# A four-layer network on one core: the first projection gets its own code, and table work on GpSimd is queued later

## The chip, the core and the metric

The kernel runs on one core of a Trainium2 chip. The core has a matrix engine (TensorE, PE in the rows, with its weight loads as PEld), two engines for elementwise work (VectorE, DVE; ScalarE, ACT), a slower general one (GpSimd, POOL) and SyncE (SP), which here only issues DMAs. Each engine takes its instructions in a fixed order and waits on semaphores for the others. The metric is the device time of one execution in microseconds; lower is better.

## The reference, cut to what matters

Sequence 256, model width 1024, all in fp32. Four layers run one after the other; each is a mixer and a feed-forward part, both on a residual `x`. Layer A (Griffin: a short convolution, two gates and a linear recurrence, beside cross-attention into `mem`) begins like this:

```python
h = rms_norm(x, norm_mix[0])
proj = h @ w_in                      # 1024 x 1536
u, gate, xq = split(proj, [512, 1024])
u = conv(u) + conv_b                 # width 4, per channel
...                                  # r, i gates, scan, gelu(gate), memory attention, w_out
x = x + concat([y_mix, y_mem]) @ w_out
x = x + square(relu(rms_norm(x, norm_mlp[0]) @ w_mlp_in[0])) @ w_mlp_out[0]
```

Layer B has forgetting attention with 8 heads in place of the recurrence, and layers C0 and C1 have a gated linear recurrence beside a three-branch sparse attention that uses rotary tables.

## The kernel before, in words

**Matmuls.** Every large product is made from fp32 numbers split into a high and a low part, each of a type that the matrix engine takes in one pass: hi·hi + lo·hi + hi·lo, three matmuls for each tile (`tri_mm`, L419 to L423, whose three lines L421, L422 and L423 are high·high, high·low-of-the-weight and low·high). The low part is exact: low = number − high.

**Weights.** The weights lie in DRAM as four streams (`sA` for layer A and so on) of pieces of 128 x 1024, 512 KB each. `load` (L351) brings them into a ring of five buffers `wr` on SP's queue; `ahead` (L363) splits a piece into `wh` (ScalarE copy, L343) and `wl` (VectorE subtraction, L344), up to `SPLIT_AHEAD` = 3 pieces ahead of the one in use. The first piece is loaded and split in two halves (`HALVES`).

**The norm.** `norm_b` handles 128 rows of `x`: eight transposes on the matrix engine (L508) in two banks of four, then for each 128 columns a ScalarE copy scaled by the norm's gain (`h` high, L511) and a VectorE step for the low part (L512). The row scale 1/rms comes from a ScalarE square with a sum (L521), two small VectorE steps (L522, L527) and a power on GpSimd (L523), and is applied after the projection.

**The first projection.** `layer_a` (L1132) loads the gate matrices (`load_small`, tile `mV`, 512 KB), spawns the norm of both blocks, and calls `proj_xt` (L630), which goes through `proj_x` (L567): four pieces, for each of the two blocks of rows 4 pieces x 2 halves x 3 matmuls of 512 columns, 48 in all. Then it scales the result (`xt`, L636) and transposes it back (L639). `griffin_consts` (L832) makes small constants from `lam` (eleven VectorE steps in `softplus_neg`, two power and log steps, and four more). The second projection (the gate half, again 48 matmuls on pieces 4 to 7), the memory projections and the output follow.

**What sets the order.** The program text gives priorities; a list scheduler of the framework decides, before the run, the order of each engine's queue. It moves an instruction ahead of earlier text where it holds it to be ready. So in the rows the square (L521) stands ahead of the copies of block 0, the matmuls of the two blocks are interleaved, and `nsa_consts` (L1223: rotary tables for layer C, sixteen GpSimd products), whose text stands in the feed-forward part of layer B for C0 and of C0 for C1, runs in the middle of layer A for C0, and in the mixer of C0 for C1.

**The start.** `setup` (L448) warms the matrix engine with three matmuls of 256 columns on zeros (L462; each shows as two instructions), and issues on SP: `x` block 0 in two halves, three pieces of weights (`FIRST` = 3, four DMAs), `x` block 1 in two halves. At most a fixed number of DMAs is under way, after which SP waits for an earlier one to land.

Of the kernel before, what the change touches and what calls it, by code (L numbers as in the profile page):

```python
# [16 lines left out]
T = 256  # L17
# [259 lines left out]
class K:  # L277
    def __init__(self, ctx, tc, a, stages):
        self.tc, self.nc, self.a = tc, tc.nc, a
        P = lambda name, bufs, **kw: ctx.enter_context(tc.tile_pool(name=name, bufs=bufs, **kw))  # L280
        self.cp = P("consts", 1)
        self.wp = P("wts", 1)
        self.hp = P("hid", 1)
        self.ps = P("psum", 8, space=bass.MemoryType.PSUM)
        self.wk = None
        self.uid = 0
        self.seq = []
        for s in stages:
            o = 0
            for j, w in enumerate(WIDTHS[s]):  # L290
                plain = s[0] == "C" and 11 <= j < 27 and j % 2 == 0
                self.seq.append((s, o, w, plain))
                o += 128 * w
        self.n_raw = self.n_split = self.n_use = 0
        self.raws, self.parts = {}, {}
        self.now, self.chains, self.marks = 0.0, [], set()


    def t(self, shape, dt=F32, tag=None, bufs=1, pool=None):
# [36 lines left out]
    def copy(self, eng, out, in_):  # L336
        if eng == "a":
            self.nc.scalar.activation(out, in_, AF.Copy)  # L338
        else:
            self.nc.vector.tensor_copy(out, in_)  # L340

    def split(self, src, hi, lo):
        self.nc.scalar.activation(hi, src, AF.Copy)  # L343
        self.nc.vector.tensor_tensor(lo, src, hi.bitcast(F32), op=OP.subtract)  # L344


    def cuts(self, i, w):
# [14 lines left out]

    def ahead(self):  # L363
        self.load(self.n_use + RAW_AHEAD)
        while self.n_split < min(len(self.seq), self.n_use + SPLIT_AHEAD):
            _, _, w, plain = self.seq[self.n_split]
            t = self.raws.pop(self.n_split)
            if plain:
                self.parts[self.n_split] = (t, None)
            else:  # L370
                self.uid += 1
                h = self.wp.tile([128, 1024], F32R, name=f"wh_{self.uid}", tag="wh", bufs=PART_BUFS)
                l = self.wp.tile([128, 1024], F32R, name=f"wl_{self.uid}", tag="wl", bufs=PART_BUFS)
# [11 lines left out]

    def power(self, m, n, p=128):
        r = self.t([128, 8], tag="rs_r", bufs=8, pool=self.hp)
        self.nc.gpsimd.tensor_tensor(r[:p, :n], m[:p, :n], self.mhalf[:p, :n], op=OP.pow)
        return r[:p, :n]

    def rstd(self, ss, n, d, fold, p=128, eps=EPS):
# [56 lines left out]
    def setup(self):  # L448
        nc, a = self.nc, self.a
        self.mhalf = self.cp.tile([128, 8], F32, name="mhalf")  # L450
        nc.vector.memset(self.mhalf, -0.5)
        self.epsn = self.cp.tile([128, 3], F32, name="epsn")
        for j, n in enumerate((1, 64, 128)):
            nc.vector.memset(self.epsn[:, j:j + 1], EPS * n)
        self.X = [self.cp.tile([128, D], F32, name=f"x{b}") for b in range(2)]
        self.consts = self.cp.tile([128, CONSTS.n], F32, name="consts_t")
        self.cols = self.cp.tile([128, COLS.n], F32, name="cols_t")
        warm = self.t([128, D], tag="n_sq", pool=self.hp)
        nc.vector.memset(warm[:, 0:512], 0.0)
        p = self.bank([128, 512])  # L460
        for _ in range(WARM):
            nc.tensor.matmul(p[:, 0:256], warm[:, 0:128], warm[:, 0:256], start=True, stop=True)  # L462
        w = self.t([128, 8], tag="rs_m", bufs=4, pool=self.hp)
        nc.scalar.activation(w, self.mhalf, AF.Ln, scale=-2.0)
        nc.scalar.dma_start(self.consts[:, 0:128], a["consts"][:, 0:128])
        nc.scalar.dma_start(self.cols, a["cols"])
        self.ident = self.con("ident")
        for b in range(2):
            for n in range(2):
                c = slice(512 * n, 512 * n + 512)  # L470
                nc.sync.dma_start(self.X[b][:, c], a["x"][128 * b:128 * b + 128, c])
            if b == 0:
                self.load(FIRST)

# [20 lines left out]
    def new_h(self, tag):  # L495

        z = self.t([128, 8, 2, T], F32R, tag=tag, pool=self.hp if tag == "h" else None)
        return z[:, :, 0], z[:, :, 1], z

    def norm_b(self, x, hn, b, wait, between=()):  # L500
        nc = self.nc
        yield wait
        g, c = self.col(hn.name), slice(128 * b, 128 * b + 128)
        for n in range(2):
            p = self.bank([128, 4, 128])
            for j in range(4):
                k = 4 * n + j
                nc.tensor.transpose(p[:, j], x[:, 128 * k:128 * k + 128], self.ident)  # L508
            for j in range(4):
                k = 4 * n + j  # L510
                nc.scalar.activation(hn.h[0][:, k, c], p[:, j], AF.Copy, scale=g[:, k:k + 1])  # L511
                nc.vector.scalar_tensor_tensor(hn.h[1][:, k, c], p[:, j], g[:, k:k + 1], hn.h[0][:, k, c].bitcast(F32),  # L512
                                               op0=OP.mult, op1=OP.subtract)
# [4 lines left out]
        yield self.lat["stat"]  # L518
        s = hn.s[b]
        sq = self.t([128, D], tag="n_sq", pool=self.hp)  # L520
        nc.scalar.activation(sq, x, AF.Square, scale=1.0 / 32, accum_out=s[:, 0:1])  # L521
# [45 lines left out]
    def proj_x(self, hn, done):  # L567

        w = [self.piece() for _ in range(4)]
        for b in range(2):  # L570
# [11 lines left out]
            done(b, o)  # L582
            self.tick(0)

    def proj_n(self, hn, n, done):

        w = [self.piece() for _ in range(3)]
# [39 lines left out]
            done(i, o)  # L627
            self.tick(0)

    def proj_xt(self, hn, scale=False):  # L630

        o = [self.bank([128, 2, T]) for _ in range(2)]

        def chain(b, p):
            z = self.t([128, 512], tag="xt")
            self.nc.scalar.activation(z, p, AF.Copy, scale=hn.s[b][:, 1:2] if scale else 1.0)  # L636
            yield self.lat["copy"]
            for j in range(4):
                self.nc.tensor.transpose(o[j // 2][:, j % 2, 128 * b:128 * b + 128], z[:, 128 * j:128 * j + 128],  # L639
                                         self.ident)  # L640
# [1 line left out]

        self.uid += 1
        name = f"xt{self.uid}"
        self.proj_x(hn, lambda b, p: self.spawn(chain(b, p), f"{name}.{b}"))
        return o, (f"{name}.0", f"{name}.1")

    def out_begin(self):
# [483 lines left out]
    def layer_a(self, after):  # L1132
        self.lat = LAT["A"]
        with self.phase("mix_a"):
            self.mem_tag = ("g_a", "g_th")
            self.load_small("A", "mV")
            h = self.norm("norm_mix0")
            if EARLY:
                self.join("norm_mix0.0")
            banks, marks = self.proj_xt(h, True)  # L1140
            self.griffin_consts()
            hm = self.mem_h("norm_mem0", MEM_A)
            g = self.t([128, 4, T], tag="g_g")
            y = self.new_y()
# [23 lines left out]
    def layer_b(self, after):  # L1168
# [24 lines left out]
            self.join("mem1")  # L1193
            self.out_last(self.ys(y, 4, 8), self.to_norm("norm_mlp1"))
        with self.phase("ffn_b"):
            self.tables = self.nsa_consts(0)
            self.ffn_a(self.h_next, after)


# [451 lines left out]
    def layer_c(self, l, after):  # L1651
# [25 lines left out]
            self.out_last(self.ys(y, 4, 8), self.to_norm(f"norm_ffn_2{l}"))  # L1677
        with self.phase(f"ffn_c{l}"):
            if l == 0:
                self.tables = self.nsa_consts(1)  # L1680
            self.ffn_2(self.h_next, after)


# [6 lines left out]
          "rms4o": 3.2, "qf": 1.8, "lev0": 2.54, "win": 0.45, "cmp": 1.06, "cmpk": 6.5},  # L1690
}
RAW_AHEAD, RAW_BUFS = 6, 5
FIRST = 3
WARM = 3
HALVES = 1
EARLY = True
MEM_A, MEM_B = 5.81, 15.14
SPLIT_AHEAD, PART_BUFS = 3, 7
NSA_SCALE_ENG = "v"
# [35 lines left out]
```

## Time and profile before

| | us |
|---|---|
| median of 3 runs (1262.37 to 1262.92) | 1262.4 |
| the profiled execution | 1262.7 |
| its span, first to last instruction | 1260.9 |
| TensorE busy | 1250.3 (99%) |
| VectorE / ScalarE / GpSimd busy | 871.2 / 731.8 / 78.5 |
| mean granted TensorE clock | 0.998 |

The profiled execution lasts 1.8 us longer than its span, and lies 0.3 us above the median. Matmuls are pipelined: one of 512 columns is drawn with some 0.39 us, but the next starts 0.23 us later when nothing is waited for. So the busy share says less than the distance from one start to the next, and a pause on the matrix engine is a gap in the starts.

### The profile page before, as it was taken

To read this page: it belongs to the slowest core of one execution; us is meant where nothing else is said; L and a number is where in the kernel's file an instruction comes from. 1 tells how busy PE (TensorE), PEld (TensorE's weight loads), DVE (VectorE), ACT (ScalarE), POOL (GpSimd) and SP (SyncE) were. 2 spreads that over 40 slices of the span, in tenths; PEclk is the share of its full clock that TensorE was granted. 3 is DMA by queue.
4 is the path that set the end of the run, shared out by engine and by line. 5 is a ranking of instruction groups with operands and counts; after the bars stand their busy time and mean duration, and the time that the engine had idled before them with its cause. 6 is when DMAs were issued, how large, how long until landed. Compare 5 with 4: busy or idle time off the path is not lost.

```text
span 1260.9 us, 19719 instructions
## 1 busy us (share of the span) xinstructions
PE 1250.3 (99%) x7442; PEld 1036.0 (82%) x7442; DVE 871.2 (69%) x1502; ACT 731.8 (58%) x1273; POOL 78.5 (6%) x122
## 2 busy tenths in 40 slices
PE   8999999999999999999999999999999999999998
PEld 6888888888878888888876788888888778888887
DVE  7786766658665766666778778666676886776663
ACT  8966544448665744445566666545455774654541
POOL 0310000001200000000410000000021000000000
PEclk9999999999999999999999999999999999999999
DMA  9554666645533565554573345555545523655550
GB/s 345 170 184 144 191 193 189 187 147 202 180 118 103 185 200 189 194 185 139 186 226 126 102 159 193 194 188 188 192 156 186 207 77 126 201 200 185 193 190 34
DMA packets 61870, 219.29 MB, mean 174 GB/s; under 512 B 6992, under 2 KB 7888, under 8 KB 61776
## 3 DMA queue, kind: packets, MB, share of 16 engines
q1 hardware_dynamic: 61488, 217.88, 52.2%
q8 instruction: 58, 0.95, 0.3%
q14 instruction: 36, 0.29, 0.1%
q10 hardware_dynamic: 288, 0.16, 0.0%
HBM read 216.96 MB, written 1.05 MB: 173 GB/s over the span
## 4 chain that ended last, share of the span: by engine, by line
PE 92%; ACT 4%; DMA 1%; DVE 1%; issue 1%; POOL 0%; DVEq 0%; ACTq 0%
PE ps L610 22%; PE ps L421 16%; PE ps L423 16%; PE ps L422 16%; PE ps L611 11%; ACT wh L343 1%; PE ps L508 1%; PE ps L1495 1%; PE ps L993 1%; PE ps L1423 1%; PE ps L1551 1%; PE ps L825 1%; PE ps L1357 1%; DMA x<-in_x_dram 1%; DMA wr<-in_sC_dram 0%
## 5 line engine op out<-in xcount | busy, mean ns | idle before, releaser
L344 DVE TENSOR_TENSOR wl<-wr,wh 128x1024 fp32r<-128x1024 f32 (+1 forms) x391 | 474.0, 1216 | 239.0 <-ACT wh L343 237.1
L343 ACT ACTIVATE wh<-wr 128x1024 fp32r<-128x1024 f32 (+1 forms) x391 | 410.3, 1054 | 335.0 <-PE ps L610 178.8
L610 PE MATMUL ps<-h,wh 128*128 128x512 f32 x1216 | 430.9, 395 | 0.0
L611 PE MATMUL ps<-h,wl 128*128 128x256 f32 x1216 | 342.9, 282 | 0.0
L610 PEld LDWEIGHTS ps<-h,wh 128*128 128x128 f32 x1216 | 228.4, 188 | 52.5 <-ACT pw_z L338 0.8
L611 PEld LDWEIGHTS ps<-h,wl 128*128 128x128 f32 x1216 | 228.6, 188 | 1.7
L421 PE MATMUL ps<-wh,ff_h 128*128 128x512 f32 x432 | 169.2, 392 | 0.0
L423 PE MATMUL ps<-wh,ff_l 128*128 128x512 f32 x432 | 168.6, 390 | 0.0
L422 PE MATMUL ps<-wl,ff_h 128*128 128x512 f32 x432 | 168.4, 390 | 0.0
L421 PE MATMUL ps<-wh,h 128*128 128x512 f32 (+1 forms) x336 | 135.3, 403 | 1.5 <-ACT wh L343 1.0
L422 PE MATMUL ps<-wl,h 128*128 128x512 f32 (+1 forms) x336 | 129.7, 386 | 0.4 <-DVE wl L344 0.2
L423 PE MATMUL ps<-wh,h 128*128 128x512 f32 (+1 forms) x336 | 129.4, 386 | 0.0
L423 PEld LDWEIGHTS ps<-wh,ff_l 128*128 128x128 f32 x432 | 81.1, 188 | 17.3
L421 PEld LDWEIGHTS ps<-wh,ff_h 128*128 128x128 f32 x432 | 81.1, 188 | 17.1
L422 PEld LDWEIGHTS ps<-wl,ff_h 128*128 128x128 f32 x432 | 81.1, 188 | 15.3
L421 PEld LDWEIGHTS ps<-wh,h 128*128 128x128 f32 x336 | 63.5, 189 | 16.8 <-issue 2.5
L423 PEld LDWEIGHTS ps<-wh,h 128*128 128x128 f32 x336 | 63.4, 189 | 13.5 <-DVE h L512 0.2
L422 PEld LDWEIGHTS ps<-wl,h 128*128 128x128 f32 x336 | 63.5, 189 | 12.5 <-DVE wl L344 1.3
L511 ACT ACTIVATE h<-ps,cols_t 128x128 fp32r<-128x128 f32 x128 | 43.7, 364 | 47.7 <-PE ps L508 36.8
L614 DVE TENSOR_TENSOR pw_o<-ps,pw_z 128x256 f32<-128x256 f32 x152 | 63.3, 417 | 8.1 <-ACT pw_z L338 8.1
L338 ACT ACTIVATE pw_z<-ps 128x256 f32<-128x256 f32 x152 | 55.9, 368 | 14.4 <-PE ps L611 14.0
L523 POOL TENSOR_TENSOR n_st<-n_st,mhalf 128x1 f32<-128x1 f32 x20 | 16.4, 821 | 688.2 <-DVE n_st L522 681.1
(329 smaller groups left out, 1434.0 us busy)
## 6 DMA issues: line engine op xcount, KB each, us to landing
wr<-in_sC_dram SPq DMA_DIRECT2D x212, 512.0 KB, 4.0
wr<-in_sB_dram SPq DMA_DIRECT2D x96, 512.0 KB, 3.6
wr<-in_sA_dram SPq DMA_DIRECT2D x91, 512.0 KB, 4.4
wr<-in_sC_dram SPq DMA_DIRECT2D x4, 420.0 KB, 3.9
x<-in_x_dram SPq DMA_DIRECT2D x4, 256.0 KB, 5.2
out_dram<-x SPq DMA_DIRECT2D x3, 256.0 KB, 2.0
wr<-in_sC_dram SPq DMA_DIRECT2D x2, 280.0 KB, 3.3
wr<-in_sA_dram SPq DMA_DIRECT2D x2, 256.0 KB, 4.7
```

The lines of the kernel that those rows point to most:

```text
L338: self.nc.scalar.activation(out, in_, AF.Copy)
L343: self.nc.scalar.activation(hi, src, AF.Copy)
L344: self.nc.vector.tensor_tensor(lo, src, hi.bitcast(F32), op=OP.subtract)
L421: mm(out, st[0], mv[0], start=start, stop=False)
L422: mm(out, st[0], mv[1], start=False, stop=False)
L423: mm(out, st[1], mv[0], start=False, stop=stop)
L508: nc.tensor.transpose(p[:, j], x[:, 128 * k:128 * k + 128], self.ident)
L511: nc.scalar.activation(hn.h[0][:, k, c], p[:, j], AF.Copy, scale=g[:, k:k + 1])
L523: nc.gpsimd.tensor_tensor(s[:, 1:2], s[:, 0:1], self.mhalf[:, 0:1], op=OP.pow)
L610: mm(p, wh[:, c], both[:, k], start=k == 0, stop=False, skip_group_check=True)
L611: mm(p[:, 0], wl[:, c], hi[:, k], start=False, stop=k == 7, skip_group_check=True)
L614: self.nc.vector.tensor_tensor(out, p[:, 0], z, op=OP.add)
```

## The change

The first projection of layer A gets its own function, `proj_first`, with the order of the matrix engine, ScalarE and VectorE pinned to the text (`keep` ties an instruction behind the one traced before it on its engine): transposes of block 0, three small matmuls, pieces 0 and 1 for block 0, transposes of block 1, pieces 0 and 1 for block 1, then pieces 2 and 3 for both blocks in turn. No piece beyond the one in use is split in it. `x`'s second block is issued after two pieces in place of three, a fourth warming matmul of 64 columns is added, the VectorE steps of `griffin_consts` are queued behind the last split of the function, and both calls of `nsa_consts` are queued on GpSimd behind the last power step traced so far.

```diff
+    def keep(self, ins):
+        if self.strict:
+            self.tc.keep_in_program_order(ins)
...
-        while self.n_split < min(len(self.seq), self.n_use + SPLIT_AHEAD):
+        while self.n_split < min(len(self.seq), self.n_use + self.split_ahead):
...
-        r = self.t([128, 8], tag="rs_r", bufs=8, pool=self.hp)
-        self.nc.gpsimd.tensor_tensor(r[:p, :n], m[:p, :n], self.mhalf[:p, :n], op=OP.pow)
+        r = self.t([128, 8], tag="rs_r", bufs=8, pool=self.hp)
+        self.last_pow = self.nc.gpsimd.tensor_tensor(r[:p, :n], m[:p, :n], self.mhalf[:p, :n], op=OP.pow)
...
+    def proj_first(self, hn, done):
+        nc = self.nc
+        mm = nc.tensor.matmul
+        self.strict, self.split_ahead = True, 0
+        tp, acc, w = {}, {}, {}
+        def turn(b):
+            tp[b] = [self.bank([128, 4, 128]) for _ in range(2)]
+            for k in range(8):
+                self.keep(nc.tensor.transpose(tp[b][k // 4][:, k % 4], self.X[b][:, 128 * k:128 * k + 128], self.ident))
+        def parts(b, u):
+            for k in (2 * u, 2 * u + 1):
+                self.parts_of(tp[b][k // 4][:, k % 4], hn, b, k)
+        def take(u):
+            self.split_ahead = 1
+            w[u] = self.piece()
+            self.split_ahead = 0
+        def products(b, u):
+            if u == 0:
+                acc[b] = self.bank([128, 512])
+            for j, (p, q) in enumerate(((0, 0), (1, 0), (0, 1))):
+                for k in range(2):
+                    self.keep(mm(acc[b], hn.h[p][:, 2 * u + k, 128 * b:128 * b + 128],
+                                 w[u][q][:, 512 * k:512 * k + 512], start=u == j == k == 0, stop=u == 3 and j == 2 and k == 1))
+        turn(0)
+        for k in range(3):
+            self.keep(mm(self.idle[:, 0:64], self.X[0][:, 512:640], self.X[0][:, 512:576], start=True, stop=True))
+        for u in range(2):
+            parts(0, u)
+            take(u)
+            products(0, u)
+        turn(1)
+        for u in range(2):
+            parts(1, u)
+            products(1, u)
+        for u in range(2, 4):
+            parts(0, u)
+            take(u)
+            parts(1, u)
+            products(0, u)
+            self.stat(self.X[u - 2], hn, u - 2)
+            if u == 3:
+                done(0, acc[0])
+            products(1, u)
+        done(1, acc[1])
+        self.marks.update(f"{hn.name}.{m}{b}" for m in ("", "s") for b in range(2))
+        self.strict, self.split_ahead = False, SPLIT_AHEAD
...
-            h = self.norm("norm_mix0")
-            if EARLY:
-                self.join("norm_mix0.0")
-            banks, marks = self.proj_xt(h, True)
-            self.griffin_consts()
+            h = self.new_norm("norm_mix0")
+            banks, marks = self.proj_xt(h, True, self.proj_first)
+            with self.tc.issue_after(self.last_low.ins):
+                self.griffin_consts()
...
-            self.tables = self.nsa_consts(0)
+            with self.tc.issue_after(self.last_pow.ins):
+                self.tables = self.nsa_consts(0)
...
-                self.tables = self.nsa_consts(1)
+                with self.tc.issue_after(self.last_pow.ins):
+                    self.tables = self.nsa_consts(1)
...
-FIRST = 3
-WARM = 3
+FIRST = 2
+WARM = (256, 256, 256, 64)
 HALVES = 1
-EARLY = True
```

`parts_of` is L511 and L512 with `keep`, and `stat` is L519 to L531 of `norm_b`, moved into functions; `split` keeps both its steps and remembers the low one as `last_low`. `proj_xt` now takes the two banks `o` when the first transposes back are traced, not ahead of the projection.

## Rows read from the trace of the kernel before

**Rows 1.** The page: the span, and each engine's busy time and share.

```profile
span 1260.9 us, 19719 instructions
PE 1250.3 (99%) x7442; PEld 1036.0 (82%) x7442; DVE 871.2 (69%) x1502; ACT 731.8 (58%) x1273; POOL 78.5 (6%) x122
```

**Rows 2.** Windows: from:to and length, busy us of each engine, clock, DMA share, GB/s.

```profile
6.80:12.20 5.40, 4.03 (x18) 2.36 (x18) 4.26 (x9) 4.66 (x11) 0.21 (x1) 1.00 1.03 403
12.20:23.00 10.80, 10.80 (x51) 8.50 (x50) 10.47 (x28) 9.66 (x19) 0.54 (x1) 1.00 0.95 359
24.00:57.00 33.00, 32.81 (x160) 26.91 (x159) 27.21 (x51) 32.71 (x63) 11.02 (x25) 1.00 0.65 226
```

**Rows 3.** Timeline of the matrix engine: start, us, engine, line, out<-in, [idle before].

```profile
4.27 1.92 PE L508 MATMUL ps<-consts_t,x 128*128 128x128 f32 x8
...
12.97 0.40 PE L422 MATMUL ps<-wl,h 128*128 128x512 f32 x1
...
20.07 0.60 PE L639 MATMUL ps<-consts_t,xt 128*128 128x128 f32 x4
20.42 0.48 PE L421 MATMUL ps<-wh,h 128*128 128x512 f32 x1
...
21.91 0.39 PE L421 MATMUL ps<-wh,h 128*128 128x512 f32 x1
22.14 0.39 PE L422 MATMUL ps<-wl,h 128*128 128x512 f32 x1
```

**Rows 4.** Timeline of ScalarE and VectorE in the same stretch.

```profile
8.88 1.06 ACT L343 ACTIVATE wh<-wr 128x1024 fp32r<-128x1024 f32 x1 [0.65 <-DMA wr<-in_sA_dram]
...
9.97 1.22 DVE L344 TENSOR_TENSOR wl<-wr,wh 128x1024 fp32r<-128x1024 f32 x1 [1.01 <-ACT wh L343]
...
17.55 1.21 DVE L344 TENSOR_TENSOR wl<-wr,wh 128x1024 fp32r<-128x1024 f32 x1
...
20.55 2.36 DVE L344 TENSOR_TENSOR wl<-wr,wh 128x1024 fp32r<-128x1024 f32 x2
```

**Rows 5.** Groups by shape, 0 to 24 us: count, busy, mean ns, idle before.

```profile
L344 DVE TENSOR_TENSOR wl<-wr,wh 128x1024 fp32r<-128x1024 f32 x7 | 8.5, 1220 | 1.1 <-ACT wh L343 1.0
L343 ACT ACTIVATE wh<-wr 128x1024 fp32r<-128x1024 f32 x8 | 8.3, 1055 | 0.7 <-DMA wr<-in_sA_dram 0.7
L511 ACT ACTIVATE h<-ps,cols_t 128x128 fp32r<-128x128 f32 x16 | 5.2, 363 | 0.5 <-DVE h L512 0.4
```

**Rows 6.** Timeline: issue of x's second block on SP, and who waited for it.

```profile
4.16 0.96 SPq L471 DMA_DIRECT2D x<-in_x_dram  x2
...
10.88 0.42 PEld L508 LDWEIGHTS ps<-consts_t,x 128*128 128x128 f32 x4 [0.45 <-DMA x<-in_x_dram]
```

**Rows 7.** Layer C0's pause: timeline, and a window as in rows 2.

```profile
660.78 1.06 ACT L343 ACTIVATE wh<-wr 128x1024 fp32r<-128x1024 f32 x1 [1.23 <-DMA wr<-in_sC_dram]
...
665.30 0.33 PE L1551 MATMUL ps<-g_g,g_c 128*32 128x32 f32 x16 [1.76 <-ACT g_c L1521]
...
665.50:669.00 3.50, 3.50 (x43) 1.94 (x30) 2.14 (x7) 3.02 (x11) 0.00 (x0) 0.51 0.96 359
```

**Rows 8.** Timeline beside GpSimd's tables (window as in rows 2), and around the named L388.

```profile
38.07 1.62 DVE L344 TENSOR_TENSOR wl<-wr,wh 128x1024 fp32r<-128x1024 f32 x1 [0.59 <-ACT wh L343]
34.20:39.85 5.65, 5.65 (x28) 4.76 (x27) 4.29 (x11) 5.65 (x16) 5.61 (x18) 1.00 0.03 11
...
362.86 1.01 POOL L388 TENSOR_TENSOR rs_r<-rs_m,mhalf 128x4 f32<-128x4 f32 x1 [6.53 <-DVE rs_m L415]
...
722.23 1.01 POOL L388 TENSOR_TENSOR rs_r<-rs_m,mhalf 128x4 f32<-128x4 f32 x1
724.65 2.37 DVE L344 TENSOR_TENSOR wl<-wr,wh 128x1024 fp32r<-128x1024 f32 x2
726.93 0.68 DVE L344 TENSOR_TENSOR yl<-ps,yh 128x512 fp32r<-128x512 f32 x1
728.63 0.40 PE L423 MATMUL ps<-wh,yl 128*128 128x512 f32 x1
```

More of the change, by code (lines that the diff above doesn't have):

```diff
@@ L296, in __init__ @@
         self.now, self.chains, self.marks = 0.0, [], set()
+        self.split_ahead, self.strict = SPLIT_AHEAD, False
     def t(self, shape, dt=F32, tag=None, bufs=1, pool=None):
@@ L340, in copy @@
             self.nc.vector.tensor_copy(out, in_)
+    def keep(self, ins):
+        if self.strict:
+            self.tc.keep_in_program_order(ins)
     def split(self, src, hi, lo):
-        self.nc.scalar.activation(hi, src, AF.Copy)
-        self.nc.vector.tensor_tensor(lo, src, hi.bitcast(F32), op=OP.subtract)
+        self.keep(self.nc.scalar.activation(hi, src, AF.Copy))
+        self.last_low = self.nc.vector.tensor_tensor(lo, src, hi.bitcast(F32), op=OP.subtract)
+        self.keep(self.last_low)
     def cuts(self, i, w):
@@ L459, in setup @@
         nc.vector.memset(warm[:, 0:512], 0.0)
-        p = self.bank([128, 512])
-        for _ in range(WARM):
-            nc.tensor.matmul(p[:, 0:256], warm[:, 0:128], warm[:, 0:256], start=True, stop=True)
+        self.idle = p = self.bank([128, 512])
+        for n in WARM:
+            nc.tensor.matmul(p[:, 0:n], warm[:, 0:128], warm[:, 0:n], start=True, stop=True)
         w = self.t([128, 8], tag="rs_m", bufs=4, pool=self.hp)
@@ L498, in new_h, with parts_of @@
         return z[:, :, 0], z[:, :, 1], z
+    def parts_of(self, p, hn, b, k):
+        g, c = self.col(hn.name)[:, k:k + 1], slice(128 * b, 128 * b + 128)
+        hi, lo = hn.h[0][:, k, c], hn.h[1][:, k, c]
+        self.keep(self.nc.scalar.activation(hi, p, AF.Copy, scale=g))
+        self.keep(self.nc.vector.scalar_tensor_tensor(lo, p, g, hi.bitcast(F32), op0=OP.mult, op1=OP.subtract))
     def norm_b(self, x, hn, b, wait, between=()):
@@ L509, in norm_b @@
             for j in range(4):
[L510 to L513, printed above, removed]
+                self.parts_of(p[:, j], hn, b, 4 * n + j)
             self.work(0.45)
@@ L518, in norm_b, with stat @@
         yield self.lat["stat"]
+        self.stat(x, hn, b)
+    def stat(self, x, hn, b):
+        nc = self.nc
         s = hn.s[b]
         sq = self.t([128, D], tag="n_sq", pool=self.hp)
-        nc.scalar.activation(sq, x, AF.Square, scale=1.0 / 32, accum_out=s[:, 0:1])
+        self.keep(nc.scalar.activation(sq, x, AF.Square, scale=1.0 / 32, accum_out=s[:, 0:1]))
         nc.vector.tensor_scalar(s[:, 0:1], s[:, 0:1], EPS, None, op0=OP.add)
@@ L583, in proj_x @@
             self.tick(0)
+    def proj_first(self, hn, done):
+        nc = self.nc
+        mm = nc.tensor.matmul
[42 more added lines that the diff above has]
+        self.strict, self.split_ahead = False, SPLIT_AHEAD
     def proj_n(self, hn, n, done):
@@ L628, in proj_w2, with proj_xt @@
             self.tick(0)
-    def proj_xt(self, hn, scale=False):
-        o = [self.bank([128, 2, T]) for _ in range(2)]
+    def proj_xt(self, hn, scale=False, proj=None):
+        o = [] if proj else [self.bank([128, 2, T]) for _ in range(2)]
         def chain(b, p):
@@ L637, in chain @@
             yield self.lat["copy"]
+            if not o:
+                o.extend(self.bank([128, 2, T]) for _ in range(2))
             for j in range(4):
@@ L644, in proj_xt @@
         name = f"xt{self.uid}"
-        self.proj_x(hn, lambda b, p: self.spawn(chain(b, p), f"{name}.{b}"))
+        (proj or self.proj_x)(hn, lambda b, p: self.spawn(chain(b, p), f"{name}.{b}"))
         return o, (f"{name}.0", f"{name}.1")
```

1 line of the change is left out of this document (removed).

## The prediction, made before the result was known

> **What bounds the kernel now.** I first read each engine's busy time on the page: TensorE is busy for 1250.3 of the 1260.9 us, the next engine, VectorE, for 871.2 [rows 1]. So almost any edit off TensorE is worth nothing by itself; what is left to win is about 10 us of idle time, plus matmuls that ran slowly. Next come the stretches by window: from 6.80 to 12.20 TensorE is busy for 4.03 of 5.40 us, from 12.20 on for every microsecond [rows 2]. The reader is to see two regimes. Before 12.2 us the start is limited by arrivals; after it, by matmuls one after the other. The change acts in the first, and touches two later places, at 360 and 720 us, where GpSimd's tables go. The third view is the later pauses; the costliest, in layer C0, is weighed below.
>
> The measure for the head is how much earlier the second projection begins. In before its first matmul starts at 21.91 [rows 3]. From 12.97, with 12 of the first projection's 48 matmuls started, TensorE never stops: 36 matmuls, and the four transposes back of block 0, which put 0.35 between one start and the next [rows 3], take 8.94 us. That is 8.59 / 36, or 0.24 us for each.
>
> **The change part by part.**
>
> *What the head waits for.* In before piece 1 of the weights is copied from 8.88, when its DMA has landed, and its low part is taken from 9.97 to 11.19 [rows 4]. The change leaves the three first DMAs of weights (two halves and piece 1) ahead of `x`'s second block, so 11.19 stands. In the new order the last two matmuls of piece 1 for block 0 need that low part: they start at 11.19 and end the block's first part at about 11.7. Pinned behind them are eight transposes; eight of them are drawn with 1.92 at 4.27, ahead of the rise of the clock [rows 3], so I take half of that, 0.9, and the last ends at about 12.6. A scaled copy takes 0.36 [rows 5] and follows the first bank of four, so block 1's first product starts at about 12.8. Then 12 matmuls and 16 transposes stand behind TensorE, as at 12.97 in before: a lead of about 0.15 us.
>
> *From there.* 36 matmuls at 0.24, less what the interleaving costs before (0.23 is the plain distance of two starts, as 21.91 to 22.14 shows [rows 3]): 36 x 0.232 = 8.35, with 0.1 for a stall at piece 2. The second projection then begins at 21.25, against 21.91 less the 0.35 of the transposes back, 21.56, if those come later in the new order. The two bounds of the head are so 0.15 and 0.31; I take 0.25, since the second includes a dense run that I assume.
>
> *`x`'s second block one piece earlier.* TensorE waits 0.45 us for it in before [rows 6]. It now lands one piece of 512 KB sooner; at the 403 GB/s of this stretch [rows 2] that is about 1.3 us. But the transposes that use it are pinned behind 11.7, later than their 10.88 of before [rows 6]. So the earlier landing is worth nothing: it is covered by the wait for piece 1's low part. Its price falls on piece 2, which now lands behind it, at about 12.7. Block 1's products on pieces 0 and 1, 12 matmuls, run from 12.8 to 15.6, and the first low product of piece 2 stands four matmuls later, at 16.5. ScalarE has block 1's first four parts and block 0's next two ahead of piece 2, six copies from 12.4 on; at 0.26 a copy (the drawn 0.36 less the 0.1 by which successors overlap) that is 14.0; then come the copy, 1.06, and the low part, 1.22 [rows 5], overlapping by 0.1: 16.1. The cover is 0.4, and the 0.1 above is charged for it; if it is gone, each tenth that piece 2 is later is a tenth of a pause. I bound that by 0.5.
>
> *Four warming matmuls and three fillers of 64 columns.* They stand where TensorE waits anyway: cold ones before its first transpose at 4.27, and warm or cold ones between the eighth transpose and the first product [rows 3]. [...] Zero, with 0.1 both ways for the moment of the rise.
>
> *Pinned engines, no split ahead.* In before ScalarE and VectorE run up to three pieces ahead: the low part of piece 4 is there at 18.76 (17.55 + 1.21) and those of pieces 6 and 7 by 22.91 [rows 4], while piece 4's first low product starts at 22.14 [rows 3]. So the slack is 22.14 - 18.76 = 3.4 us. In the new code only four pieces are split inside the function; I expect three splits to be left over at its end. ScalarE needs 3 x 0.95 (a drawn 1.06, next start 0.1 before its end) = 2.9 us for them, VectorE 3 x 1.14 = 3.4. Between 12.20 and 23.00 ScalarE has 1.1 us idle and VectorE 0.3; between 24 and 57 they have 0.3 and 5.8 [rows 2]. So the slack of 3.4 is spent to the last half microsecond, without a pause of TensorE. I take zero; the bounds are 0 and 3.4 us.
>
> *`griffin_consts` behind the last split.* Some fifteen steps of 0.15 us on VectorE leave the head and go behind; who waits is the first gate, at 28 us and later. Hidden, if the splits are.
>
> *The tables on GpSimd.* `nsa_consts(0)` leaves 34.2 to 39.85, where GpSimd works for 5.6 us and a split on VectorE takes 1.62 us beside it instead of 1.22 [rows 5, 8]. It goes behind the power step of 362.86 [rows 8]; no product waits for it until layer C0. The gain is 0.4 on VectorE, where there was slack, so zero. `nsa_consts(1)` leaves the mixer of C0 and goes behind the step of 722.23, so to about 723.3 to 728.9. There two splits stand, drawn 2.37 for both (1.2 each, so undisturbed), and `yl` ends at 727.61 for a matmul at 728.63: 1.0 us of cover [rows 8]. By the 0.4 of the row above, three VectorE steps lose up to 1.2, so 0.2 are lost at worst; without cover, 1.2.
>
> [...]
>
> *The pause of C0.* [...] With the tables gone from the mixer of C0, its splits are up to 0.5 us less delayed, and piece and pause may come that much earlier. I take 0.1.
>
> **The sum.** Head -0.25, C0 -0.1, behind 722 +0.1: -0.25, so 1262.45 in place of the profiled 1262.7, and 1262.2 beside the median of 1262.4. Its own range, from the bounds above (head -0.4 to +0.4, C0 -0.5 to 0, 722 0 to +0.2): 1261.5 to 1263.0.
>
> **The rivals.**
>
> *The split backlog (slower).* If ScalarE and VectorE come out of the head four splits behind, not three, or the constants go first, the low part of piece 4 comes later than 22.14 and TensorE waits for it and each that follows. One more split costs 1.14 of VectorE, three with the constants' 15 x 0.15 more: 1.4 to 3.4 us, around 1264.6. It decides from the moment at which piece 4's low part ends after 21.9. For it speaks that ScalarE is busy for 32.71 of 33.00 us after 24 us [rows 2], so that lost time is not made up there; against it that the new function gives them idle time at its waits for the piece in use, which unpinned later splits may fill. 0.20.
>
> *The slow stretch of C0 goes away (faster).* A pause a little shorter, or shifted, and the clock stays at full: 1.7 off, 1260.5: 0.12. If the pause too shrinks, by its 1.76, it is 1258.8: 0.06. For them, the tables leave C0's mixer; against them, the wait starts with a DMA.
>
> [...]
>
> *GpSimd blocks VectorE at 723 (slower).* A full block of the splits for 5.6 us, less the cover of 1.0: +4.6, 1266.8. The row with 0.4 speaks against it: 0.03. [...]
>
> **How the numbers follow.** My forecast 0.54, and the rivals 0.20, 0.12, 0.06, 0.05, 0.03. The likeliest is 1262.2. The range takes in the backlog up to 1264.9 and the loss of the slow stretch at 1260.5, with 0.6 for their sizes, 1259.9; it leaves out the two ends, about 0.17. A change of 0.2%, 2.5 us, is about what a measurement of this kernel can tell from none. Below 1259.9 lies 0.08, above 1264.9 the block and a quarter of the backlog, 0.09; 0.83 is the rest.
>
> **What would show it.** Right: block 1's first product at 12.8, the second projection's first matmul at 21.2 to 21.5, no gap in TensorE between 21 and 29, and the same pause and slow stretch near 665. Wrong: a wait for `wl` in the second projection (backlog); a granted clock of 1.00 through 669 (slow stretch gone); splits of over 2 us at 724 (block). A second projection that begins later than 21.9 would refute the head's sum.

## The result, and the profile after

The changed kernel takes 1269.4 us (median of five runs, 1267.7 to 1269.9) where the kernel before takes 1262.4: a ratio of 1.0055, with a 95% interval of 1.0040 to 1.0069, so it is slower by 5 to 9 us, 0.4 to 0.7%. The profiled execution has a span of 1268.1 us, 7.2 more than before. My 1262.2 with a range up to 1264.9 is wrong: the time lies 4.5 us above the upper end, and I had forecast no change.

The page's first lines and the windows that answer to [rows 1, 2] (columns as there) show where to look:

```profile
span 1268.1 us, 19733 instructions
PE 1252.9 (99%) x7450; PEld 1036.3 (82%) x7450; DVE 871.0 (69%) x1502; ACT 732.4 (58%) x1273; POOL 79.9 (6%) x122
...
6.80:12.20 5.40, 3.65 (x12) 2.16 (x13) 3.45 (x6) 2.56 (x5) 0.00 (x0) 1.00 1.02 395
12.20:23.00 10.80, 8.22 (x34) 5.24 (x33) 5.18 (x14) 6.63 (x16) 0.55 (x1) 1.00 0.81 309
24.00:57.00 33.00, 31.34 (x149) 24.45 (x150) 27.87 (x68) 32.11 (x63) 7.04 (x9) 1.00 0.59 191
```

The loss is in the head. From 12.20 to 23.00 TensorE was busy for all of 10.80 us; now for 8.22. ScalarE and VectorE are idle there too, 4.2 and 5.6 us: nobody is the bound, they wait for each other. After 24 us TensorE is idle for a further 1.5 us.

TensorE's pauses, from its timeline (the last column is idle before, and who released it; L625 are the new function's products, L428 the second projection, L708 the transposes back):

```profile
17.67 1.20 PE L625 MATMUL ps<-wh,h 128*128 128x512 f32 x4 [0.57 <-ACT wh L349]
...
22.70 1.19 PE L625 MATMUL ps<-wh,h 128*128 128x512 f32 x4 [1.64 <-ACT wh L349]
...
27.13 0.48 PE L428 MATMUL ps<-wh,h 128*128 128x512 f32 x1
...
29.42 0.66 PE L708 MATMUL ps<-consts_t,xt 128*128 128x128 f32 x4 [0.64 <-ACT xt L703]
```

The second projection starts at 27.13; in before at 21.91 [rows 3]: 5.2 us. The start of the 13th product moved by 0.3 only (13.31 against 12.97), the end of the second projection's products by 6.9, and the first matmul of the memory attention at 76.86 (now 83.86) by 7.0. Behind it nothing more than 0.2 is added.

Why ScalarE came late with `wh` is seen on ScalarE and, for one row, VectorE (L511 scaled copy, L512 low step, L349 and L350 split, L535 square):

```profile
12.89 0.37 ACT L511 ACTIVATE h<-ps,cols_t 128x128 fp32r<-128x128 f32 x1 [2.52 <-PE ps L609]
13.68 0.37 ACT L511 ACTIVATE h<-ps,cols_t 128x128 fp32r<-128x128 f32 x1 [0.42 <-DVE h L512]
14.47 0.37 ACT L511 ACTIVATE h<-ps,cols_t 128x128 fp32r<-128x128 f32 x1 [0.42 <-DVE h L512]
15.25 0.62 ACT L511 ACTIVATE h<-ps,cols_t 128x128 fp32r<-128x128 f32 x2 [0.42 <-DVE h L512]
16.30 0.37 ACT L511 ACTIVATE h<-ps,cols_t 128x128 fp32r<-128x128 f32 x1 [0.42 <-DVE h L512]
16.57 1.05 ACT L349 ACTIVATE wh<-wr 128x1024 fp32r<-128x1024 f32 x1
...
19.17 0.37 ACT L511 ACTIVATE h<-ps,cols_t 128x128 fp32r<-128x128 f32 x1 [1.30 <-DVE h L512]
19.43 1.05 ACT L535 ACTIVATE n_sq<-x 128x1024 f32<-128x1024 f32 x1
...
21.34 0.37 ACT L511 ACTIVATE h<-ps,cols_t 128x128 fp32r<-128x128 f32 x1 [0.50 <-DVE h L512]
21.60 1.05 ACT L349 ACTIVATE wh<-wr 128x1024 fp32r<-128x1024 f32 x1
...
17.65 1.23 DVE L350 TENSOR_TENSOR wl<-wr,wh 128x1024 fp32r<-128x1024 f32 x1 [0.59 <-ACT wh L349]
18.79 0.35 DVE L512 SCALAR_TENSOR_TENSOR h<-ps,cols_t,h 128x128 fp32r<-128x128 f32 x1
```

Two things are to be seen. First a ping-pong: a copy waits for the low step of the column before it, and so copies stand 0.79 us apart, not 0.26. One pair does not wait (15.25, two in 0.62): its second copy reads another PSUM bank. Where a split stands between on VectorE (17.65) the wait is 1.30. Second, the square of 1.05 us at 19.43, pinned between copies that piece 3 needs. The pause of 1.64 at 22.70 is reached by going back from 21.60: 0.50, the square, 1.30.

What I did not weigh is which bank each step reads. The waits of 0.42 are for the other engine's step on the same bank, and the second copy of 15.25, on another bank, goes ahead without one. They are waits for semaphores of the program; what the chip would do without them no run here shows.

The other two places of the change are as forecast. C0's pause and slow stretch are there as in [rows 7] (timeline, window), and GpSimd's tables behind 722 us, now 7 us later, stop no matmul:

```profile
672.48 0.33 PE L1620 MATMUL ps<-g_g,g_c 128*32 128x32 f32 x16 [1.73 <-ACT g_c L1590]
...
674.00:677.50 3.50, 3.50 (x13) 2.10 (x14) 3.14 (x11) 1.70 (x7) 0.00 (x0) 0.52 0.71 247
...
731.80 1.58 POOL L1308 TENSOR_TENSOR n_rk<-consts_t,rows_t 128x64 f32<-128x64 f32 x2
733.35 1.23 POOL L1309 TENSOR_TENSOR n_rc<-consts_t,rows_t 128x32 f32<-128x32 f32 x1
...
731.97 2.50 DVE L350 TENSOR_TENSOR wl<-wr,wh 128x1024 fp32r<-128x1024 f32 x2
```

The two splits take 2.50 in place of 2.37 [rows 8]; it is GpSimd's products that take longer beside them, 1.23 for one that takes 0.25 with VectorE idle (at 735.38). At 38.07 in before a split on VectorE lost 0.4 beside GpSimd's products, 1.62 for 1.22 [rows 5, 8].

### The profile page after: what moved, and what is told of

It reads as the page before. It is cut to its first block, busy times and chain, and to the rows that moved or that the text cites. A ratio compares the mean times of both kernels' runs of the same rounds, so it can differ in the third digit from the quotient of the medians.

```text
span 1268.1 us, 19733 instructions
## 1 busy us (share of the span) xinstructions
PE 1252.9 (99%) x7450; PEld 1036.3 (82%) x7450; DVE 871.0 (69%) x1502; ACT 732.4 (58%) x1273; POOL 79.9 (6%) x122
## 3 DMA queue, kind: packets, MB, share of 16 engines
HBM read 216.96 MB, written 1.05 MB: 172 GB/s over the span
## 4 chain that ended last, share of the span: by engine, by line
PE 91%; ACT 1%; DVE 1%; issue 0%; DMA 0%; POOL 0%; DVEq 0%; ACTq 0%
PE ps L677 22%; PE ps L428 16%; PE ps L430 16%; PE ps L429 16%; PE ps L678 11%; PE ps L521 1%; PE ps L1564 1%; PE ps L1062 1%; PE ps L1492 1%; PE ps L1620 1%; PE ps L894 1%; PE ps L1426 1%; PE ps L860 0%; PE ps L1080 0%; DMA wr<-in_sC_dram 0%
## 5 line engine op out<-in xcount | busy, mean ns | idle before, releaser
L350 DVE TENSOR_TENSOR wl<-wr,wh 128x1024 fp32r<-128x1024 f32 (+1 forms) x391 | 473.5, 1216 | 241.6 <-ACT wh L349 241.0
L349 ACT ACTIVATE wh<-wr 128x1024 fp32r<-128x1024 f32 (+1 forms) x391 | 410.2, 1055 | 335.4 <-PE ps L677 178.8
L428 PE MATMUL ps<-wh,ff_h 128*128 128x512 f32 x432 | 169.2, 392 | 0.0
L428 PE MATMUL ps<-wh,h 128*128 128x512 f32 (+1 forms) x320 | 128.8, 403 | 0.0
L430 PE MATMUL ps<-wh,h 128*128 128x512 f32 (+1 forms) x320 | 123.3, 385 | 0.0
L429 PE MATMUL ps<-wl,h 128*128 128x512 f32 (+1 forms) x320 | 123.2, 385 | 0.0
L428 PEld LDWEIGHTS ps<-wh,ff_h 128*128 128x128 f32 x432 | 81.1, 188 | 17.2
L511 ACT ACTIVATE h<-ps,cols_t 128x128 fp32r<-128x128 f32 x128 | 44.2, 364 | 57.3 <-PE ps L521 36.8
L428 PEld LDWEIGHTS ps<-wh,h 128*128 128x128 f32 x320 | 60.6, 189 | 14.2 <-issue 2.7
L430 PEld LDWEIGHTS ps<-wh,h 128*128 128x128 f32 x320 | 60.4, 189 | 12.8
L429 PEld LDWEIGHTS ps<-wl,h 128*128 128x128 f32 x320 | 60.7, 190 | 10.7
L512 DVE SCALAR_TENSOR_TENSOR h<-ps,cols_t,h 128x128 fp32r<-128x128 f32 x128 | 42.2, 345 | 26.6 <-ACT h L511 25.5
```

What stands on the lines that cost most here:

```text
L349: self.keep(self.nc.scalar.activation(hi, src, AF.Copy))
L350: self.last_low = self.nc.vector.tensor_tensor(lo, src, hi.bitcast(F32), op=OP.subtract)
L428: mm(out, st[0], mv[0], start=start, stop=False)
L429: mm(out, st[0], mv[1], start=False, stop=False)
L430: mm(out, st[1], mv[0], start=False, stop=stop)
L511: self.keep(self.nc.scalar.activation(hi, p, AF.Copy, scale=g))
```

## The experiments

My theories: **W**, the waits of copies for low steps of the same bank; **Q**, the pinned squares; rivals, TensorE's own fixed order, the text order, the first loads, and **C**, the constants queued behind. Times are device us; a ratio is against runs of before made beside that kernel's, and since runs of one kernel spread over 4 to 7 us (before: 1259.1 to 1264.9 in one set of 25 runs, 1259.5 to 1266.6 in another of 29) verdicts go by ratios. "13th" and "49th" are the starts of those products in the profiled execution, the 49th being the first of the second projection.

| kernel | median | ratio to before (95%) | 13th | 49th |
|---|---|---|---|---|
| before | 1262.4 | 1 | 12.97 | 21.91 |
| after | 1269.4 | 1.0055 (1.0040 to 1.0069) | 13.31 | 27.13 |
| e1_pairs | 1266.1 | 1.0033 (1.0022 to 1.0044) | 13.80 | 23.43 |
| e2_stat | 1268.5 | 1.0055 (1.0033 to 1.0076) | 13.19 | 25.55 |
| e3_free | 1263.9 | 1.0016 (1.0005 to 1.0027) | 12.72 | 22.04 |
| e4_tables | 1262.0 | 0.9999 (0.9987 to 1.0011) | 13.47 | 22.28 |
| e5_both | 1263.7 | 1.0015 (1.0006 to 1.0024) | 13.05 | 22.45 |
| e6_all | 1264.2 | 1.0020 (1.0011 to 1.0029) | 13.51 | 23.42 |
| e7_pe | 1268.1 | 1.0043 (1.0029 to 1.0057) | 14.35 | 26.92 |
| e8_ad | 1268.2 | 1.0047 (1.0032 to 1.0062) | 11.99 | 25.35 |
| e9_const | 1264.0 | 1.0017 (1.0006 to 1.0028) | 13.86 | 23.28 |
| e10_free_const | 1263.0 | 1.0012 (0.9998 to 1.0026) | 13.83 | 22.65 |
| e11_loads | 1262.8 | 1.0009 (0.9998 to 1.0019) | 13.68 | 22.49 |
| e12_after_const | 1268.0 | 1.0047 (1.0029 to 1.0065) | 14.20 | 28.03 |
| e13_loads | 1263.2 | 1.0014 (1.0004 to 1.0025) | 12.94 | 22.35 |
| e14_fours | 1263.4 | 1.0015 (1.0006 to 1.0024) | 12.69 | 22.23 |
| e15_free | 1261.5 | 1.0006 (0.9997 to 1.0015) | 13.56 | 22.34 |

The last two columns come from one profile each. In six of these (e1_pairs, e4_tables, e9_const to e12_after_const) the granted clock is at half for 3.4 us somewhere between 8.4 and 12.9 us (0.50 from 8.40 to 11.80 in e1_pairs, 0.50 from 9.00 to 12.40 in e4_tables), and in e7_pe from 17.0 to 20.4 (0.51); there the starts are later, in e4_tables, whose head is that of before, by 0.50 and 0.37 us, and differences of that size say nothing. A mark further on agrees with the ratios: the first matmul of the memory attention, at 76.86 in before, starts 7.0 us later in after, 6.3 in e2_stat, 4.5 in e1_pairs, 2.15 in e5_both, 1.0 in e14_fours, 0.65 in e3_free and 0.45 in e15_free.

**Copies in pairs (e1_pairs).**

```diff
-            for k in (2 * u, 2 * u + 1):
-                self.parts_of(...)            # copy, low, copy, low
+            for e in "ad":                    # copy, copy, then low, low
+                for k in (2 * u, 2 * u + 1):
+                    ...
```

> The changed kernel, with one edit: the pinned order of each two columns of the norm is copy, copy on ScalarE and then low, low on VectorE, where it was copy, low, copy, low. Theory W (the loss comes from the scaled copy of ScalarE waiting for VectorE's low step of the column before it, 0.42 us each time, eight times in the head of the changed kernel): half of these waits go, block 1's four first copies end about 0.9 us earlier, piece 2's copy starts near 15.2 us in place of 16.57, and the second projection starts 3 to 4 us earlier, at 23 to 24 us in place of 27.13; the time is 1265 to 1266.5 beside 1269.4. Theory Q (the loss comes from the two squares of 1.15 us that are pinned ahead of the copies for piece 3 and of the second xt): under 1 us is gained, 1268.4 or more.

1266.1: 3.2 us less than after by the medians, 2.8 by the ratios. Piece 2's copy starts at 15.70 instead of 16.57, the 49th product at 23.43 instead of 27.13. W is right in sign, and the time lies in its range, in part by luck. One reading in my expectation was wrong: of the eight waits in after five are of 0.42 and three longer (0.50, 0.76, 1.30), 4.7 us in all, and not half of them but all except one, of 0.68, are gone. With the head shorter, the split backlog appears that I had named as a rival; the second projection now waits for low parts (TensorE's timeline):

```profile
24.71 0.51 PE L429 MATMUL ps<-wl,h 128*128 128x512 f32 x1 [0.81 <-DVE wl L350]
...
29.09 0.50 PE L429 MATMUL ps<-wl,h 128*128 128x512 f32 x1 [0.87 <-DVE wl L350]
```

The first of these low parts is late because VectorE has waited 1.15 us, up to 23.29, for GpSimd's step of the constants that stand ahead of the split at 23.44.

**Squares early (e2_stat).**

```diff
         turn(1)
+        for b in range(2):
+            self.stat(self.X[b], hn, b)
...
-            self.stat(self.X[u - 2], hn, u - 2)
```

> The changed kernel, with one edit: both squares with their sums are traced, and pinned on ScalarE, behind block 1's transposes, where ScalarE is idle from 10.4 to 12.9 us in the changed kernel, and not in the loop over pieces 2 and 3. Theory Q (the squares' place costs): piece 3's copy starts 1.1 us earlier than 21.60, the 0.64 wait of the second transposes back for xt goes, and 1.5 to 2.5 us are gained: 1267 to 1268. Theory W (the waits between the copies and the low steps carry the loss): 0 to 1 us, and up to 0.5 is lost if block 1's first copy comes behind the second square.

The 49th product starts 1.58 us earlier, at 25.55, as Q has it, but the ratio is that of after. With four runs its interval is wide, 1.0033 to 1.0076. In the profile the gain is given back at once. This is from the list of waits from 28 to 36 us:

```profile
PE ps L942 <- ACT xt L704: 2.1, 1, 2.1
```

The order behind the head, which the scheduler sets, is another one: on ScalarE an `xt` copy now stands at 33.00 behind four steps of the convolution, and TensorE waits for it for 2.1 us. That the earlier head led to this order is my reading; no run tests it.

**Nothing pinned (e3_free).**

```diff
-        self.strict, self.split_ahead = True, 0
+        self.strict, self.split_ahead = False, 0
```

> The changed kernel without any pinning (the function's text order only gives priorities; no split ahead, tables, first loads and constants as in the change). If the pinned order is the cause, whatever its detail, ScalarE's copies run 0.26 us apart in pairs again, the second projection starts at 21.5 to 23.5, and the time is 1262 to 1264. If the text order itself is the cause (block 1 late, one block's products after the other's, no split ahead), little is gained: 1267 or more.

1263.9; the 49th product is at 22.04, 0.13 later than before. On ScalarE block 1's eight copies stand in a row without a wait:

```profile
10.98 2.20 ACT L511 ACTIVATE h<-ps,cols_t 128x128 fp32r<-128x128 f32 x8
```

So the pinning, and not the new text order, carries most: 1.0055 becomes 1.0016.

**The tables alone, on the kernel before (e4_tables).**

```diff
-            self.tables = self.nsa_consts(0)
+            with self.tc.issue_after(self.last_pow.ins):
+                self.tables = self.nsa_consts(0)
```

(and the same for the second call)

> The kernel before, with one part of the change: both table sets of layer C queued on GpSimd behind the power step traced last. My prediction has this part at -0.1 to +0.2 us, 1262.3 to 1262.6, with the half-clock stretch near 668 us still there. The rival (GpSimd blocks VectorE at 723 us) has 1264 to 1267; that the stretch at half clock goes has 1260.5.

0.9999 (0.9987 to 1.0011): nothing that can be measured, as forecast.

**Pairs and early squares together (e5_both).**

> The changed kernel with both edits, copies in pairs and the squares early. If the two causes add (3.3 us from the pairs, 1.6 us at the second projection from the squares), the second projection starts at 22 to 22.5 us and the time is 1263.5 to 1265, what is left being the waits for low parts of pieces 4 and 5 (0.81 and 0.87 us in the run with pairs alone). If the split backlog takes the place of what is removed, the second projection starts earlier but waits more for low parts: 1265.5 to 1266.5, no better than pairs alone.

1263.7, and 1.0015: of the 0.0055, 0.0040 is back, some 5 us. The squares, whose place showed no gain alone, are worth 0.0018 here beside pairs (1.0033 to 1.0015; the two intervals just touch). The waits for low parts of e1_pairs are gone. Of the copies' waits for a low step one is left, 0.68 at the second pair; the 0.29 is a wait for the transposes (ScalarE):

```profile
12.63 0.62 ACT L617 ACTIVATE h<-ps,cols_t 128x128 fp32r<-128x128 f32 x2 [0.29 <-PE ps L609]
13.93 1.14 ACT L617 ACTIVATE h<-ps,cols_t 128x128 fp32r<-128x128 f32 x4 [0.68 <-DVE h L619]
```

**All four copies of a bank first (e14_fours).** Squares early, and

```diff
+            if u % 2:
+                return
+            for e in "ad":
+                for k in range(2 * u, 2 * u + 4):
```

> The changed kernel with squares early and the four copies of each bank ahead of its four low steps (both for pieces 0 and 1, or 2 and 3, at once). If the wait of a copy hangs on the bank that it shares with the low step before it, no copy of block 1 waits for a low step in the head, where pairs still wait 0.68 us once a bank; the waits go from the rows. The time: block 0's first product comes 0.5 us later (two more copies ahead of piece 0), block 1's last first-bank copies 0.5 earlier: 1263.2 to 1264.5. If copies still wait for low steps of another bank, the wait hangs on something else.

No copy of the head waits for VectorE any more. Block 1's eight copies, on two banks, follow each other 0.25 apart, and the first low step comes 0.03 us after the fourth copy's end (13.42):

```profile
12.27 2.18 ACT L619 ACTIVATE h<-ps,cols_t 128x128 fp32r<-128x128 f32 x8 [0.29 <-PE ps L609]
...
13.45 2.17 DVE L621 SCALAR_TENSOR_TENSOR h<-ps,cols_t,h 128x128 fp32r<-128x128 f32 x8 [1.00 <-ACT h L619]
```

Both directions are seen: a copy waits for low steps of its bank that stand ahead of it, a low step for the copies of its bank that do. So the wait hangs on the bank, which is one tile of the program here. The time is as with pairs, 1.0015: the one wait of 0.68 that pairs leave costs nothing that can be measured.

**Copies of both blocks before the split (e6_all).** As e5_both, with `parts(1, u)` ahead of `take(u)`.

> As the last (pairs, squares early), and in pieces 2 and 3 the columns of both blocks are copied before the piece is split, so that block 1's low steps don't stand behind the split's 1.22 us on VectorE (a 1.30 us wait in the changed kernel). Theory W: 0 to 0.7 us less than the last, 1263 to 1264.5, as piece 2's copy comes 0.5 us later and its first products are not ready earlier. The rival: the split is the later of the two and each moves the products by 0.5: 0.5 to 1 us more than the last.

1.0020 beside 1.0015: no gain, and the 49th product comes 1 us later; of the two expectations the rival's is nearer, though the intervals overlap.

**TensorE alone pinned, and its complement (e7_pe, e8_ad).** The `keep` calls are taken from `split`, `parts_of` and `stat`; or, in e8_ad, from transposes, fillers and products.

> The changed kernel with TensorE's order pinned alone; ScalarE's and VectorE's are left to the scheduler. If the pinned order of ScalarE and VectorE is the cause (theories W and Q), the copies come in pairs and the squares in pauses as without any pinning: the second projection at 21.5 to 23, 1262.5 to 1264.5. If TensorE's fixed order (block 1's transposes behind block 0's pieces 0 and 1) is the cause, 1267 or more.

> The changed kernel with ScalarE's and VectorE's order pinned and TensorE's left to the scheduler, the complement of the last. Theories W and Q: 1267 to 1270, with the waits of a copy for the low step before it (0.42 us each) as in the changed kernel, though block 1's transposes come earlier. If TensorE's order is the cause: 1262 to 1264.

Here I missed. Pinning ScalarE and VectorE alone gives 1.0047, as expected, with eight waits of copies for low steps (four of 0.42, the others 0.50, 0.85 and twice 1.30). But TensorE's order alone gives 1.0043, where I had 1262.5 to 1264.5. Its timeline shows the products in a fixed order waiting for a copy that ScalarE does later:

```profile
8.59 1.23 PE L624 MATMUL ps<-wh,h 128*128 128x512 f32 x3 [0.94 <-ACT h L510]
...
11.97 0.96 PE L624 MATMUL ps<-wh,h 128*128 128x512 f32 x3 [1.17 <-ACT h L510]
...
16.02 0.74 PE L624 MATMUL ps<-wh,h 128*128 128x512 f32 x2 [1.16 <-ACT h L510]
```

On ScalarE the copy for the second of these starts at 11.55, behind a square at 10.41. Behind these pauses the granted clock of this profile is at half for a while, so its 49th product, at 26.92, is later than the order alone makes it, by up to 1.7 us (half of 3.4; window):

```profile
17.00:20.50 3.50, 3.23 (x7) 2.29 (x8) 3.09 (x13) 3.21 (x7) 2.00 (x1) 0.51 0.81 313
```

The parts do not add: 0.0043 and 0.0047 alone, 0.0055 together, 0.0016 with neither.

**The constants not queued behind (e9_const, e10_free_const, e12_after_const).**

```diff
-            with self.tc.issue_after(self.last_low.ins):
-                self.griffin_consts()
+            self.griffin_consts()
```

on e5_both, e3_free and the changed kernel.

> The changed kernel with copies in pairs, squares early, and the small constants of the recurrence no longer queued behind the last split. Theory C (the queued constants cost: their chain VectorE, GpSimd, VectorE, ScalarE makes VectorE wait 0.91 and ScalarE 0.72 us ahead of splits and of the second xt, as the run with both edits shows at 22 us): 0.5 to 1.2 us less than that run's 1263.7, so 1262.5 to 1263.2, about even with the kernel before. If those waits lie beside other work: 1263.5 to 1264.

> The changed kernel with nothing pinned, and the constants not queued behind the last split. In the run with nothing pinned ScalarE waits 1.64 us at these constants and the time is 1263.9. Theory C: 1262.0 to 1263.2, even with the kernel before or up to 1 us above. If the constants are covered: 1263.7 to 1264.2.

> The changed kernel with the constants alone not queued behind the last split; order pinned as in the change. Theory C, if the parts add: 0.5 to 1 us less than 1269.4. If the pinned order hides them (ScalarE and VectorE have pauses enough in it; ScalarE waits 0.1 us at these constants in the changed kernel, and VectorE 0.65): 0 to 0.3 less, 1269 to 1269.5. If they now come into the pinned stretch's way: up to 0.5 more.

Theory C came from the list of waits of e3_free from 15 to 22 us: the constants go through three engines, and each waits in its place in the queue.

```profile
POOL spn L440 <- DVE spn L439: 5.7, 1, 5.7
ACT spn L449 <- DVE spn L444: 1.6, 1, 1.6
DVE spn L444 <- POOL spn L440: 0.9, 1, 0.9
```

Undone, the ratios go from 1.0015 to 1.0017, 1.0016 to 1.0012, 1.0055 to 1.0047. All changes lie within the intervals; beside pairs and early squares there is no gain, so C is not shown.

**The first loads (e11_loads, e13_loads, e15_free).**

```diff
-FIRST = 2
-WARM = (256, 256, 256, 64)
+FIRST = 3
+WARM = (256, 256, 256)
```

undone on e5_both (e13) and on e10_free_const (e15); e11 is the reverse, done alone on the kernel before.

> The kernel before with the order of the first loads (x's second block behind two pieces) and the fourth warming matmul alone. My prediction has these at nothing, 0.1 either way, plus up to 0.5 for piece 2 landing later: 1262.0 to 1262.9 beside 1262.4, or the same shift beside its own runs of before. If the later piece 2 stalls the head: +0.5 to +1.2. If x's second block is what the head of before waits for: -0.3 to -0.5.

> The changed kernel with copies in pairs and squares early, and the first loads and warming matmuls as before the change (x's second block behind three pieces, no fourth warming matmul; the three fillers stay). If the loads carry the rest: 0.6 to 1.2 us less than the 1263.7 of pairs and squares, 1262.5 to 1263.1. If the later second block now holds up the second square and block 1's copies: 0.3 to 1 more, 1264 to 1264.7. If neither: 1263.4 to 1264.

> The changed kernel with nothing pinned, the constants not queued behind, and the first loads and warming matmuls as before; left of the change are the text order of the function, no split ahead in it, the fillers and the tables. If pins, constants and loads are all that cost: 1261.5 to 1262.4 beside before's 1262, within 0.3 of it. If the text order or the missing split ahead costs too: 1262.7 to 1263.5.

Alone they give 1.0009 (0.9998 to 1.0019); undone on the pinned version 1.0014 in place of 1.0015, on the unpinned 1.0006 in place of 1.0012. No effect is clear of noise. With nothing pinned and constants and loads as before, the kernel can't be told from before: 1.0006 (0.9997 to 1.0015). It still has the new text order, the three fillers and the queued tables.

## Why the prediction was wrong, point by point

- **The bound.** That the head waits on arrivals up to 12.2 us and runs dense from there was right for before. I took "dense from there" over to the new order, and that was the error: 12.20 to 23.00 lost 2.6 us of TensorE's work.
- **The step that failed** is the schedule of copies in the part on `x`'s second block: six copies at 0.26 each, 1.6 us to piece 2's copy. They took 3.7, from 12.89 to 16.57, at 0.79 with a wait and 0.27 without. That left TensorE a pause of 0.57 at piece 2; the larger one, 1.64 at piece 3, comes of the same waits (1.30 and 0.50) and a square, and for piece 3 I had no schedule at all. The row for the wait was shown: of ScalarE's 0.5 us of idle time before the sixteen copies, 0.4 is put down to VectorE's low step [rows 5]. In before that is one wait, at 17.67, since the scheduler sets copies two and more ahead of their low steps (ScalarE and VectorE):

```profile
11.49 0.88 ACT L511 ACTIVATE h<-ps,cols_t 128x128 fp32r<-128x128 f32 x3
...
12.76 1.28 DVE L512 SCALAR_TENSOR_TENSOR h<-ps,cols_t,h 128x128 fp32r<-128x128 f32 x4
...
17.67 0.37 ACT L511 ACTIVATE h<-ps,cols_t 128x128 fp32r<-128x128 f32 x1 [0.36 <-DVE h L512]
```

  The change pins the alternation. That it costs is shown by undoing it: 1.0055 becomes 1.0033 (e1_pairs), and with the squares early 1.0055 becomes 1.0015 (e2_stat, e5_both).
- **The missing term** is the pinned squares: the change has `keep` on them and two instructions of 1.05 us in the loop; I gave them no cost at all. Alone, moving them showed no gain (e2_stat); with the ping-pong gone it is worth 0.0018, about 2.3 us.
- **A wrong assumption behind both**, which I did not write down, was that pins only fix an order that would be much the same. e7_pe shows that even TensorE's order alone costs 0.0043.
- **13th product**: 12.8 forecast, 13.31 measured. It waits on piece 1's low part (11.63 for 11.19), late by one such wait (0.76 us before the copy at 9.06), and on the copy behind the transposes. The lead of 0.15 became a lag of 0.34. The other bound of the head, 0.31, fell too: it has the transposes back behind the start of the second projection, and they came ahead of it, at 26.72.
- **The split backlog** decided nothing in the changed kernel: the second projection starts so late that the splits are there. It came up, with 0.81 and 0.87 us, once the head was shorter (e1_pairs), the first time behind the constants, as that rival's condition has it. The mechanism was right, and masked. Its price has a slip: one more split is 1.14 and 3.4 with the constants, so the lower end is 1.1, not 1.4.
- **`x`'s second block, first loads, warming**: nothing clear of noise, 1.0009 (0.9998 to 1.0019, e11_loads). The three fillers were never tested alone; e15_free has them at 1.0006. No run shows by itself the 0.1 for the moment at which the clock rises.
- **The tables**: 0.9999 (e4_tables), right as far as the noise tells. No run shows the splits blocked for the 5.6 us of the last rival: in after two of them took 2.50 us beside GpSimd's products, for 2.37 in before.
- **C0's slow stretch**: still there in the profile of after, at 674 us; the rival that it goes did not decide. No run shows the 0.1 that the sum takes off C0's pause: the pause was 1.73 us in after for 1.76 in before. Nor does one show the 1.7 us of the stretch as a time: it is an estimate, half of the 3.5 us at 0.51 [rows 7], and e4_tables, whose profile has none at C0 and one in the head, is at 0.9999. That this forecast came true is luck: of the seventeen profiles only those of before, after and e8_ad have a slow stretch there.

What stays open: pinned, with pairs and early squares, the kernel is still 0.0015 (0.0006 to 0.0024, or 0.8 to 3.0 us) above before. In e14_fours' profile 0.3 of it lies before the 49th product and 0.7 in the second projection. Neither the constants (e9_const) nor the loads (e13_loads) account for it by themselves; undoing both on the pinned kernel, or taking TensorE's pins off it, was not tried. And no version here is faster than the kernel before.

## What to carry to other kernels

Before an order is pinned, go through its neighbours on different engines that read the same PSUM bank: here an alternation "copy, low, copy, low" made two engines take turns, with copies 0.79 us apart (after), and the same steps grouped by bank ran side by side, with copies 0.25 apart (e14_fours). Cost every instruction that gets a pin, the side steps too, at its place in the queue: without the square of 1.05 us ahead of it, piece 3's copy came 1.25 us earlier (20.35 for 21.60, e2_stat). And a fixed order on one engine was here only as good as the order in which the others delivered; pinned alone, TensorE lost about as much (1.0043, e7_pe) as ScalarE and VectorE pinned alone (1.0047, e8_ad).

## What the runs showed of the hardware that I had not expected

Where the granted clock falls to half (0.50 to 0.52 in the windows) differs between profiles with the same pause. Ten of the seventeen have one such stretch of 3.4 us ahead of the program's last 2 us: at C0's pause in before, after and e8_ad, in the head in the six named under the table, at 17.0 us in e7_pe; the other seven have none. The mean granted clock of the ten profiled runs is 0.998 or 0.999, that of the seven 1.000. The windows of e4_tables, whose head is that of before, have:

```profile
9.00:12.40 3.40, 3.33 (x10) 2.38 (x11) 2.82 (x6) 3.14 (x8) 0.00 (x0) 0.50 1.04 415
665.50:669.00 3.50, 3.28 (x47) 2.12 (x48) 2.65 (x7) 3.44 (x12) 0.00 (x0) 1.00 0.94 342
```

The stretch lies in the head, and none follows the pause of 1.80 us that ends at 665.72, where before has one behind a pause of 1.76 [rows 7]. It costs what the stretch was doing: in the head, where TensorE waits anyway, the 49th product starts 0.37 us later than before (22.28), not 1.7. The clock differs between runs of one kernel, too: of the 99 runs of before beside the experiments, the 13 with a mean granted clock of 0.997 have a median of 1263.7 us, the 28 with 1.000 one of 1261.0. So part of the spread of single runs goes with the clock.

The trace's first record of the clock at full level differs as well: it lies between 4.56 (e15_free) and 6.87 us (e6_all). In before, with that record at 6.79, the eight transposes that start at 4.27 took 1.92 us; in after, with it at 5.12, those that start at 4.59 took 1.30. So a price of the clock read from one profile is a price of that profile.
